# Position bias lines written to DRAM once, read back as overlapping reversed rows and flipped by a matmul

## The chip, the core and the metric

The kernel runs on one core of a Trainium2 chip. The metric is the time of one execution on the device in microseconds (us). The engines of the core work side by side, each through its own queue in order: TensorE (matmuls; PE in the rows, its weight loads PEld), VectorE (DVE), ScalarE (ACT), GpSimd (POOL) and SyncE (SP), which here only issues transfers. Sixteen DMA engines move the data between DRAM, which holds inputs, output and scratch, and the on-chip memory SBUF. Matmul results land in PSUM, eight banks of 128 x 512 float32.

## What is computed

One decoder layer on 512 tokens of width 1024. A modulated layer norm feeds one wide input projection. From it come a gated MLP branch and three groups of eight attention heads, with windows and strides of (128, 1), (512, 4) and (2048, 16). The branches are merged by gates, projected and normalized, and a mixture of 32 experts, four for each token, follows. The part that matters here is the position bias of the attention: it depends on the distance of query and key alone.

```python
band = (didx >= 0) & (didx <= span)                 # didx = qi + 128 - ki
bucket = t5_bucket(jnp.clip(didx, 0, None) * dilation)
bias = bias_table[bucket].astype(jnp.float32).transpose(2, 0, 1)
logits = einsum('brnqhd,brnkhd->brnhqk', qb, kb) * (Dh ** -0.5) + bias
logits = where(valid, logits, NEG_INF)
...
p = exp(logits - m)
o = einsum('brnhqk,brnkhd->brnqhd', p / den, vb)
```

## The kernel before

The program consists of a front (about the first 650 us) and the experts. In the front, the modulation vectors are computed from `w_ada`, the normalized input is transposed and split into two float32r parts (`hh`, `hl`), and every projection is done as three float32r matmuls (`mm3`, L165 to L167). Weights come as tiles of 1 MB (`wload`, L114, pool `land`, four buffers, issued by SP). ScalarE and VectorE split each tile into two halves (L109 and L110, pool `splA`, four buffers).

For each head group g, `attention(g)` projects v, k and q (`projN`, `projT`). Four PSUM accumulators named `mm` collect a projection and are emptied into `t2` tiles: v and q by ScalarE (L480), k by VectorE (L482). Between these projections of the groups 1 and 2, `mod_row` (L451) computes a modulation row: four tiles of `w_ada`, each multiplied and added on VectorE (L221 and L223 in `mod_acc`), then two plain float32 matmuls with a column of ones (L457).

Then the heads are worked off. A step j takes `nh` heads: 2 of width 256 in group 0, 4 of width 128 in the others, so that there are 4, 2 and 2 steps, eight in all. Each step needs one bias tile of 128 queries x 512 values. For each of four blocks of queries, TensorE computes scores (L510) in one of two PSUM tiles named `at`, VectorE scales them and adds the bias (L513), takes the maximum (L515), ScalarE takes the exponential (L519), TensorE transposes (L524), VectorE copies (L526), TensorE multiplies by v (L532) and ScalarE copies out (L534).

The bias is a Toeplitz matrix, a line of values for each head read at an offset that moves by one from query to query. The lines (`fv`: 8 heads, 383 values in group 0 and 255 in the others) come from one small matmul per group (L426) and a copy (L428). L429, issued by GpSimd, writes each line 128 times to the DRAM scratch `toep`, one copy per query. `bias_tile` (L431) then reads with SP (L435): query p starts at copy p and goes back by p values, so that a row pitch of n - 1 gives the slanted read. A bias tile has two buffers, and VectorE reads it at L513.

The order of each queue is not written out by hand here. A planner of the framework fixes it at build time, from program order as priority, from dependences and free buffers, and from modelled durations. On the chip each engine then keeps to that order, whatever the real durations are. Loads of weights, bias tiles and rows share the SP queue.

The experts run in a schedule by hand: for each expert twelve 1 MB tiles of weights pass through 17 buffers, some of which are those that the front gives back (`land`, `landB`, `splA`).

Of the kernel before, what the change touches and what calls it, by code (L numbers as in the profile page):

```python
# [9 lines left out]
F32 = mybir.dt.float32  # L10
# [11 lines left out]
P = 128  # L22
# [4 lines left out]
NE = 32  # L27
# [5 lines left out]
SEGS = (383, 255, 255)  # L33
# [4 lines left out]

def host_consts():

    cst = np.zeros((P, 3 * P + NE), np.float32)
    cst[:, :P] = np.eye(P)
    cst[:, P:2 * P] = np.arange(P)
    cst[:, 2 * P:3 * P] = np.triu(np.ones((P, P)), 1)
    cst[:, 3 * P:] = 8.0 ** (np.arange(NE) % 8)
    edges = np.array([16, 22, 30, 40, 54, 73, 99, 134, 182, 246, 332, 450, 609, 825, 1117, 1513])

    def bucket(d):
        return d if d < 16 else 15 + int((edges <= d).sum())

    oh = np.zeros((33, sum(SEGS)), np.float32)
    for g, n in enumerate(SEGS):
        for u in range(n):
            t = u - 127
            if g == 0:
                d = P - t if 0 <= t <= P else -1
            elif g == 1:
                d = -4 * t if t <= 0 else -1
            else:
                d = -4 * t if t <= 0 and t % 4 == 0 else -1  # L60
            if d < 0:
                oh[32, SEG0[g] + u] = NEG
            else:
                oh[bucket(d), SEG0[g] + u] = 1.0
    sel = np.concatenate([np.eye(NE, dtype=np.float32)] * 3, 0)
    return {"cst": cst, "ohb": oh, "sel": sel}


def layer(tc, I, out, dump=None, n_exp=NE):
    nc = tc.nc  # L70
    V, S, G, PE, SP = nc.vector, nc.scalar, nc.gpsimd, nc.tensor, nc.sync
    main = ExitStack()
    dram = main.enter_context(tc.tile_pool(name="dram", bufs=1, space=DRAM))
# [5 lines left out]
    rowd = dram.tile([4, D], F32, name="rowd")  # L79
    h2d = dram.tile([T, D], F32, name="h2d")  # L80
    ysum = dram.tile([T, D], F32, name="ysum")
    toep = [dram.tile([8, P, n], F32, name=f"toep{g}") for g, n in enumerate(SEGS)]

    cst = cp.tile([P, 2 * P], F32, name="cst_s")
    SP.dma_start(cst, I["cst"][:, :2 * P])
# [26 lines left out]
    def wload(ap, pool=None, eng=SP):  # L112
        t = (pool or land).tile([P, 2048], F32, name="land")
        eng.dma_start(t.rearrange("p (k f) -> p k f", k=ap.shape[1]), ap)  # L114
        return t
# [57 lines left out]
    f = fa.enter_context(tc.tile_pool(name="f", bufs=1, side="right"))  # L173
# [14 lines left out]
    def att():  # L188
        return pA.tile([P, 512], F32, name="at", bufs=2)
# [51 lines left out]
    pb = att()  # L241
# [140 lines left out]
    pb = att()  # L382
# [25 lines left out]
    for g in range(8):  # L408
        ps = pot()
        PE.matmul(ps[:, :256].rearrange("p (n c) -> p n c", n=4), wsT[:, g], vn[:, :, 64 * g:64 * g + 64],  # L410
                  start=True, stop=True)
# [11 lines left out]
    for g in range(3):  # L423
        n = SEGS[g]
        ps = att()
        PE.matmul(ps[:8, :n], relb[:, 8 * g:8 * g + 8], ohb[:, SEG0[g]:SEG0[g] + n], start=True, stop=True)  # L426
        fv = f.tile([8, 512], F32, name="t2", bufs=22)
        S.copy(fv[:, :n], ps[:8, :n])  # L428
        G.dma_start(toep[g], fv[:, None, :n].to_broadcast([8, P, n]))  # L429

    def bias_tile(g, h0, nh, w):  # L431

        t = f.tile([P, nh, w], F32, name="bias", bufs=2)
        n = SEGS[g]
        SP.dma_start(t, bass.AP(tensor=toep[g].tensor, offset=toep[g].offset + h0 * P * n + 127,  # L435
                                ap=[[n - 1, P], [2 * P * n, nh], [1, w]]))
        return t

    yaT = b16(F32R, 2, 4, T)
# [27 lines left out]
    def attention(g, between=()):  # L467
# [27 lines left out]
        for j in range(8 // nh):  # L495

            h0 = j % 2 + 2 * nh * (j // 2)
            hs = slice(h0, h0 + 2 * nh - 1, 2)
            bt = bias_tile(g, h0, nh, w)
            for b in range(4):  # L500
                kb0 = 1 if g == 0 and b == 0 else 0
# [158 lines left out]
    f = fb.enter_context(tc.tile_pool(name="f2", bufs=1, side="right", reuse_waits="tile"))  # L660
# [10 lines left out]
    for a in range(4):  # L671
        t = wload(wov[:, 2 * a:2 * a + 2, :])
# [30 lines left out]
    tri = f.tile([P, P], F32, name="pj", bufs=2)  # L703
    SP.dma_start(tri, I["cst"][:, 2 * P:3 * P])
    pow8 = f.tile([P, NE], F32, name="pow8")
    SP.dma_start(pow8, I["cst"][:, 3 * P:])
    iota_e = iota[:, :NE]
    V.tensor_copy(trib, tri)
    oneb = f.tile([P, P], BF, name="oneb")
# [668 lines left out]
```

## Time and profile before

| | |
|---|---|
| timed runs, median (range) | 1897.74 us (1893.63 to 1898.98), 3 runs |
| profiled execution, its time | 1892.72 us |
| its span, first to last instruction | 1891.0 us |
| TensorE busy | 1740.1 us (92%) |
| VectorE, ScalarE, GpSimd busy | 547.4, 378.2, 203.4 us |
| moved by DMA | 518.99 MB, 274 GB/s in the mean |
| mean granted clock of TensorE | 0.968 of full speed |

The span is cut into 40 slices of 47.3 us on the page; a digit is the busy share of a slice in tenths. The granted clock (PEclk) is what TensorE was given of its full speed. Waits are listed as waiter, releaser, total, times, longest. A plain float32 matmul stands in the rows as two records, a float32r matmul as one. The rows show single executions, so that a duration in them may differ by a little from run to run.

### The profile page before, as it was taken

The numbers are of one execution on the slowest core, as the hardware profiler recorded it, in microseconds if no ns is written. First come the engines' busy times: TensorE is split into PE (matmuls) and PEld (weight loads), VectorE is DVE, ScalarE is ACT, GpSimd is POOL, SyncE is SP. The second block draws the span as 40 slices with busy tenths as digits, with TensorE's granted clock in tenths as the row PEclk, the third lists the DMA queues.
The fourth block names the chain that finished last, engine by engine and source line by source line (L and its number), as shares of the span: only waits on it lengthen the run. The fifth ranks groups of instructions, "written<-read, shape, count | busy, mean of one in ns | idle before, by whom it ended". The sixth has DMA issues, their size and how long they took to land. (4 is left out here: it accounts for less than half of the span.)

```text
span 1891.0 us, 20283 instructions
## 1 busy us (share of the span) xinstructions
PE 1740.1 (92%) x7574; PEld 989.6 (52%) x7574; DVE 547.4 (29%) x901; ACT 378.2 (20%) x737; POOL 203.4 (11%) x152
## 2 busy tenths in 40 slices
PE   5993999999999699999999999998899999999985
PEld 5773878888777444444444444443344444444442
DVE  7532654845267801111111111111101111111115
ACT  3530434444555310011000000010010000000001
POOL 2100000003122410010000000010000001001002
PEclk9997999999999699999999999999999999999998
DMA  8595522723225897999999999999972499949993
GB/s 282 185 94 149 206 88 81 257 69 108 93 99 174 279 379 260 361 404 405 396 399 401 371 393 378 352 400 400 404 286 88 160 393 394 388 160 327 405 372 139
DMA packets 160475, 518.99 MB, mean 274 GB/s; under 512 B 19018, under 2 KB 23426, under 8 KB 160198
## 3 DMA queue, kind: packets, MB, share of 16 engines
q1 hardware_dynamic: 146886, 490.68, 67.7%
q0 software_dynamic: 13312, 24.98, 7.3%
q8 instruction: 129, 2.11, 0.5%
q14 instruction: 148, 1.21, 0.2%
HBM read 504.15 MB, written 26.64 MB: 281 GB/s over the span
## 5 line engine op out<-in xcount | busy, mean ns | idle before, releaser
L165 PE MATMUL mm<-b,splA 128*128 128x512 f32 x352 | 139.5, 396 | 28.7 <-DVE t L482 28.7
L1079 ACT ACTIVATE ga<-ga 128x512 f32<-128x512 f32 (+1 forms) x36 | 28.7, 796 | 576.9 <-DVE ga L1078 400.8
L1131 PE MATMUL po<-land,aT 128*128 128x512 f32 x320 | 141.5, 594 | 1.1 <-DVEq L1173 1.1
L166 PE MATMUL mm<-b,splA 128*128 128x512 f32 x352 | 139.0, 395 | 0.0
L167 PE MATMUL mm<-b,splA 128*128 128x512 f32 x352 | 138.6, 394 | 0.0
L1105 PE MATMUL pu<-land,xT 128*64 128x256 f32 x1024 | 123.9, 386 | 6.3 <-DMA land<-in_w_up_dram 6.3
L1108 PE MATMUL pu<-land,xT 128*128 128x512 f32 x288 | 128.8, 592 | 0.0
L1073 PE MATMUL pg<-land,xT 128*128 128x512 f32 x288 | 126.0, 592 | 2.4 <-issue 2.4
L110 DVE TENSOR_TENSOR splA<-land,splA 128x1024 fp32r<-128x1024 f32 x70 | 87.9, 1258 | 129.0 <-ACT splA L109 124.6
L1070 PE MATMUL pg<-land,xT 128*64 128x512 f32 x504 | 118.9, 619 | 4.1 <-DMA land<-in_w_gate_dram 2.9
L1078 DVE TENSOR_SCALAR ga<-pg 128x512 f32<-128x512 f32 x44 | 30.4, 692 | 318.1 <-PE pg L1073 154.9
L1082 DVE TENSOR_SCALAR pu<-pu 128x256 f32<-128x256 f32 (+1 forms) x64 | 34.1, 533 | 290.5 <-PE pu L1108 160.9
L109 ACT CAST splA<-land 128x1024 fp32r<-128x1024 f32 x72 | 75.3, 1052 | 213.1 <-PE mm L167 171.9
L1128 PE MATMUL po<-land,aT 128*64 128x512 f32 x448 | 105.1, 607 | 7.6 <-ACT aT L1089 7.6
L1089 ACT COPY aT<-ptm 128x256 f32<-128x256 f32 (+1 forms) x64 | 28.9, 452 | 350.6 <-PE ptm L1039 350.6
L1105 PEld LDWEIGHTS pu<-land,xT 128*64 128x64 f32 x1024 | 72.9, 138 | 47.8 <-DMA land<-in_w_up_dram 9.6
L1131 PEld LDWEIGHTS po<-land,aT 128*128 128x128 f32 x320 | 59.4, 190 | 70.3 <-issue 67.9
L1026 POOL DMA_INDIRECT xrow<-h2d,gidx x32 | 33.9, 1060 | 538.3 <-PE ptm L1039 528.3
L1073 PEld LDWEIGHTS pg<-land,xT 128*128 128x128 f32 x288 | 54.6, 190 | 69.2 <-issue 66.3
L165 PEld LDWEIGHTS mm<-b,splA 128*128 128x128 f32 x352 | 66.6, 189 | 44.6 <-DVE t L482 29.1
L1108 PEld LDWEIGHTS pu<-land,xT 128*128 128x128 f32 x288 | 53.5, 190 | 66.1 <-issue 63.9
L1070 PEld LDWEIGHTS pg<-land,xT 128*64 128x64 f32 x504 | 38.2, 143 | 75.3 <-issue 66.7
(376 smaller groups left out, 2498.9 us busy)
## 6 DMA issues: line engine op xcount, KB each, us to landing
land<-in_w_up_dram SPq DMA_DIRECT2D x100, 1024.0 KB
land<-in_w_gate_dram SPq DMA_DIRECT2D x99, 1024.0 KB
land<-in_w_down_dram SPq DMA_DIRECT2D x96, 1024.0 KB
splA<-in_w_down_dram SPq DMA_DIRECT2D x32, 1024.0 KB
land<-in_w_in_dram SPq DMA_DIRECT2D x30, 1024.0 KB
splA<-in_w_gate_dram SPq DMA_DIRECT2D x29, 1024.0 KB
splA<-in_w_up_dram SPq DMA_DIRECT2D x28, 1024.0 KB
land<-in_w_ada_dram SPq DMA_DIRECT2D x24, 1024.0 KB
```

Source lines behind the costliest of these rows:

```text
L109: hi = S.copy(w[:, 0], src)
L110: return hi, eng.tensor_tensor(w[:, 1], src, w[:, 0].bitcast(F32), op=ALU.subtract)
L165: PE.matmul(o, l[0], r[0], start=start, stop=False)
L166: PE.matmul(o, l[0], r[1], start=False, stop=False)
L167: return PE.matmul(o, l[1], r[0], start=False, stop=stop)
L1070: PE.matmul(r[h], x[:, kt, :H], w[:, :, h], start=False, stop=kt == KT - 1)
L1073: PE.matmul(o[st], x[:, kt], w[:, 512 * st:512 * st + 512], start=False, stop=kt == KT - 1)
L1082: V.tensor_scalar(o, o, LIMIT, -LIMIT, op0=ALU.min, op1=ALU.max)
L1105: PE.matmul(o[st][H * h:H * h + H, :256], x[:, kt, :H], w[:, 256 * h:256 * h + 256], start=False, stop=kt == KT - 1)
L1108: PE.matmul(o[st], x[:, kt], w, start=False, stop=kt == KT - 1)
L1128: end = PE.matmul(o[0][H * n:H * n + H], a[:, 2 * st + b, H * h:H * h + H], wn, start=ft == 0, stop=ft == KT - 1)
L1131: end = PE.matmul(o[n], a[:, ft], wn, start=ft == 0, stop=ft == KT - 1)
```

## The change

The lines are written to `toep` once: the scratch is `[8, n]` instead of `[8, 128, n]`. `bias_tile` reads 128 overlapping rows, partition p starting at value p of the line, so the slant runs the other way and the queries stand in reverse order. A matmul with a reversed identity (`flip`, a new 64 KB constant that SP loads) brings them into order: from the tile to a PSUM tile of the `at` kind, from which ScalarE copies back into the same tile. The host constant `cst` gets 128 more columns for it. Each of the eight bias tiles thus has one more plain float32 matmul and one more ScalarE copy between its read and its readers.

```diff
--- before.py
+++ after.py
@@ -38,11 +38,12 @@
 
 def host_consts():
 
-    cst = np.zeros((P, 3 * P + NE), np.float32)
+    cst = np.zeros((P, 4 * P + NE), np.float32)
     cst[:, :P] = np.eye(P)
     cst[:, P:2 * P] = np.arange(P)
     cst[:, 2 * P:3 * P] = np.triu(np.ones((P, P)), 1)
-    cst[:, 3 * P:] = 8.0 ** (np.arange(NE) % 8)
+    cst[:, 3 * P:3 * P + NE] = 8.0 ** (np.arange(NE) % 8)
+    cst[:, 3 * P + NE:] = np.eye(P)[::-1]
     edges = np.array([16, 22, 30, 40, 54, 73, 99, 134, 182, 246, 332, 450, 609, 825, 1117, 1513])
 
     def bucket(d):
@@ -79,7 +80,7 @@
     rowd = dram.tile([4, D], F32, name="rowd")
     h2d = dram.tile([T, D], F32, name="h2d")
     ysum = dram.tile([T, D], F32, name="ysum")
-    toep = [dram.tile([8, P, n], F32, name=f"toep{g}") for g, n in enumerate(SEGS)]
+    toep = [dram.tile([8, n], F32, name=f"toep{g}") for g, n in enumerate(SEGS)]
 
     cst = cp.tile([P, 2 * P], F32, name="cst_s")
     SP.dma_start(cst, I["cst"][:, :2 * P])
@@ -426,14 +427,19 @@
         PE.matmul(ps[:8, :n], relb[:, 8 * g:8 * g + 8], ohb[:, SEG0[g]:SEG0[g] + n], start=True, stop=True)
         fv = f.tile([8, 512], F32, name="t2", bufs=22)
         S.copy(fv[:, :n], ps[:8, :n])
-        G.dma_start(toep[g], fv[:, None, :n].to_broadcast([8, P, n]))
+        G.dma_start(toep[g], fv[:, :n])
+
+    flip = f.tile([P, P], F32, name="flip")
+    SP.dma_start(flip, I["cst"][:, 3 * P + NE:])
 
     def bias_tile(g, h0, nh, w):
 
+        n = SEGS[g]
         t = f.tile([P, nh, w], F32, name="bias", bufs=2)
-        n = SEGS[g]
-        SP.dma_start(t, bass.AP(tensor=toep[g].tensor, offset=toep[g].offset + h0 * P * n + 127,
-                                ap=[[n - 1, P], [2 * P * n, nh], [1, w]]))
+        SP.dma_start(t, bass.AP(tensor=toep[g].tensor, offset=toep[g].offset + h0 * n, ap=[[1, P], [2 * n, nh], [1, w]]))
+        pb = att()
+        PE.matmul(pb, flip, t.rearrange("p h w -> p (h w)"), start=True, stop=True)
+        S.copy(t.rearrange("p h w -> p (h w)"), pb)
         return t
 
     yaT = b16(F32R, 2, 4, T)
@@ -703,7 +709,7 @@
     tri = f.tile([P, P], F32, name="pj", bufs=2)
     SP.dma_start(tri, I["cst"][:, 2 * P:3 * P])
     pow8 = f.tile([P, NE], F32, name="pow8")
-    SP.dma_start(pow8, I["cst"][:, 3 * P:])
+    SP.dma_start(pow8, I["cst"][:, 3 * P:3 * P + NE])
     iota_e = iota[:, :NE]
     V.tensor_copy(trib, tri)
     oneb = f.tile([P, P], BF, name="oneb")
```

## Rows read from the trace of the kernel before

**Rows 1.** The page, part 2: busy tenths in 40 equal slices of the span.

```profile
PE   5993999999999699999999999998899999999985
...
DMA  8595522723225897999999999999972499949993
```

**Rows 2.** Stretches of 10 us: length, busy us by engine, PEclk, DMA.

```profile
150.00:160.00 10.00, 0.00 (x0) 0.00 (x0) 0.00 (x0) 0.00 (x0) 0.00 (x0) 0.50 0.50 65
160.00:170.00 10.00, 0.00 (x0) 0.00 (x0) 0.00 (x0) 0.00 (x0) 0.00 (x0) 0.50 0.49 102
170.00:180.00 10.00, 7.43 (x25) 6.03 (x26) 5.55 (x7) 1.05 (x1) 0.00 (x0) 0.69 0.53 178
```

**Rows 3.** Waits of TensorE, longest: waiter, releaser, us in total, times, longest.

```profile
PE mm L165 <- DVE t L482: 28.7, 1, 28.7
```

**Rows 4.** Timeline of all engines around the hole: start us, us, what.

```profile
138.00 1.28 DVE L482 COPY t<-mm 128x512 f32<-128x512 f32 x2
...
143.50 0.39 PE L167 MATMUL mm<-b,splA 128*128 128x512 f32 x1
171.16 0.75 DVE L221 TENSOR_SCALAR q<-land,cs 128x1024 f32<-128x1024 f32 x1 [31.88 <-DMA land<-in_w_ada_dram]
...
172.56 0.80 PE L165 MATMUL mm<-b,splA 128*128 128x512 f32 x1 [28.68 <-DVE t L482]
...
176.42 0.40 PE L165 MATMUL mm<-b,splA 128*128 128x512 f32 x1
...
176.65 0.39 PE L166 MATMUL mm<-b,splA 128*128 128x512 f32 x1
...
178.73 1.28 DVE L223 SCALAR_TENSOR_TENSOR q<-land,cs,q 128x1024 f32<-128x1024 f32 x1 [3.29 <-DMA land<-in_w_ada_dram]
```

**Rows 5.** Timeline of the SP queue: issues of transfers.

```profile
132.67 0.37 SPq L114 DMA_DIRECT2D land<-in_w_ada_dram  x1
...
173.73 0.37 SPq L114 DMA_DIRECT2D land<-in_w_ada_dram  x1
...
231.94 0.37 SPq L435 DMA_DIRECT2D bias<-toep  x1
...
569.25 0.43 SPq L684 DMA_DIRECT2D row_ln_g<-in_ln_g_dram  x1
```

**Rows 6.** Transfers by issue: tile, queue, count, KB each, us to landing.

```profile
toep<-t POOLq DMA_DIRECT2D x2, 1020.0 KB, 65.7
toep<-t POOLq DMA_DIRECT2D x1, 1532.0 KB, 55.3
```

**Rows 7.** The toep tiles: their issues, and the landing of the three writes.

```profile
L429 POOL DMA_DIRECT2D toep<-t x3: 1079/1113/1337, 91.2 to 93.6; - x3
...
DMA to landing us min/median/max: 55.3/56.5/74.9
```

**Rows 8.** Longer stretches: two in the attention, one in the experts.

```profile
200.00:250.00 50.00, 50.00 (x257) 41.58 (x257) 35.50 (x62) 22.51 (x71) 0.00 (x0) 1.00 0.40 138
300.00:350.00 50.00, 49.95 (x270) 44.73 (x269) 34.03 (x49) 32.16 (x90) 1.01 (x2) 1.00 0.28 87
900.00:1000.00 100.00, 98.65 (x427) 43.55 (x426) 13.48 (x22) 8.20 (x15) 8.14 (x7) 1.00 1.02 397
```

**Rows 9.** Timeline of TensorE around a plain float32 matmul.

```profile
373.97 1.88 PE L457 MATMUL at<-q,ones 128*1 128x512 f32 x4
375.78 0.50 PE L165 MATMUL mm<-b,splA 128*128 128x512 f32 x1
```

**Rows 10.** Timeline of ScalarE: one copy of 128x512 from PSUM.

```profile
115.37 0.59 ACT L480 COPY t<-mm 128x512 f32<-128x512 f32 x1 [0.30 <-PE mm L167]
```

**Rows 11.** Stretches with a bias read alone, and with broadcast lines.

```profile
233.00:234.00 1.00, 1.00 (x5) 0.61 (x5) 1.00 (x3) 0.18 (x1) 0.00 (x0) 1.00 0.80 240
570.00:575.00 5.00, 5.00 (x19) 3.97 (x19) 2.16 (x4) 0.00 (x0) 0.00 (x0) 0.78 0.86 295
```

**Rows 12.** Timeline of VectorE: first reader of the bias tile issued at 231.94.

```profile
245.85 0.42 DVE L513 SCALAR_TENSOR_TENSOR sc<-at,bias 128x256 f32<-128x256 f32 x1
```

## Prediction

> **What bounds the kernel now.** I read the views in this order: busy shares and slices, stretches of 10 us, waits of TensorE, the timeline around the one hole, then the transfers. The slices show one hole in TensorE, the fourth slice, about 142 to 189 us, while the DMA engines go on working [rows 1]. By stretches TensorE does nothing from 150 to 170 us and is back at 170 to 180 us with a mean granted clock of 0.69 of full speed [rows 2]. The wait list names it: one wait of 28.7 us, a matmul of the next projection for the copy at L482, the largest of TensorE's list [rows 3].
>
> The timeline shows the cause [rows 4]. VectorE empties two of the four k accumulators from 138.00 on. The next instruction in its queue is L221, the first step of a modulation row, which needs a w_ada tile; it starts at 171.16 after 31.88 us of idling for that transfer. Two further L482 copies stand behind L221, so the accumulators stay full. TensorE starts its last matmul at 143.50 and the next at 172.56. The w_ada tile was issued at 132.67 [rows 5], so it took 38.5 us. The next one, issued at 173.73 [rows 5], is read at 178.73 [rows 4], 5.0 us later. What differed is the traffic: the three toep writes (one of 1532 KB, two of 1020 KB [rows 6]) were issued from 91.2 to 93.6 and took 55.3 to 74.9 us [rows 7]; if the longest is the last one, it was done near 168.5. While only they and the w_ada tile remain, the DMA engines show a share of 0.49 to 0.50 and move 65 to 102 GB/s [rows 2]. About 3 us after the last toep byte the w_ada tile is there. So the 128-fold write does not delay the bias itself; it delays a weight tile, which delays VectorE's queue, which delays TensorE.
>
> Behind the hole TensorE is full again (50.00 and 49.95 us of two later stretches of 50 us [rows 8]), and it is not catching up: the work behind it moves by what the hole costs. The expert stage later has TensorE at 98.65 of 100 us with a DMA share of 1.02 [rows 8]; its tiles are loaded into buffers that the earlier stages give back, so its start moves with them. I therefore carry the whole gain to the end.
>
> **The change part by part.**
> *Toep writes.* 3.57 MB become 24 lines of 1020 or 1532 bytes, 28 KB in all, and the long traffic goes. The w_ada tile of 132.67 should then land after about 5.0 us, at 137.7, before L221 comes up at 139.28 (two copies, 1.28 us, from 138.00). The slack is 1.6 us. What comes next is VectorE's wait for the second w_ada tile, 3.29 us before 178.73 [rows 4]; it exists already, TensorE ran beside it, and it stays hidden. So the 28.68 us wait goes.
> *Clock.* In the idle stretch the granted clock falls to 0.50 [rows 2], the lower of its two levels (1.2 against 2.4 GHz). From 172.56 to 176.42 nine matmuls start some 0.43 us apart, and behind them the step is 0.23 us [rows 4]. 3.86 minus 9 times 0.23 is 1.8 us. Gone as well. Together 30.5 us.
> *Flip matmuls, 8.* A plain float32 128x512 matmul is two records on TensorE. Two of them at L457 hold it from 373.97 to 375.78 [rows 9], 0.90 us each. L457 has one column of weights and the flip 128, but weight loads run beside the stream. 8 times 0.90 is 7.2 us, and as TensorE is full there [rows 8], all of it counts. Lower bound 0 (if they fall into other idle time, of which there is little), upper bound 8 times 1.0 us, since the matmul behind the change of operand takes 0.50 instead of 0.39 us [rows 4, 9], 8.0 us.
> *ScalarE copies, 8.* PSUM to SBUF, 128x512: 0.59 us [rows 10], 4.7 us in all. ScalarE is busy 22.51 and 32.16 of 50 us in the stretches concerned [rows 8], so I cost them at nothing. The cover is TensorE's projection matmuls; without it, a score step would start 0.59 plus 0.90 us later for each tile, 12 us over eight.
> *The at buffers.* pb takes one of the two PSUM buffers of the scores from matmul to copy, about 1.5 us a tile. A score step that waits for it costs TensorE nothing while projection matmuls are there to run; between 0 and 8 times 1.5 = 12 us, and I take 1 us, near the lower end, because TensorE is full in these stretches with the same two buffers [rows 8].
> *Bias reads, 8.* Same bytes (256 KB) and row lengths as before. One alone, issued at 231.94 [rows 5], shows as 240 GB/s in the microsecond from 233 to 234 us [rows 11], which is nearly all of its 256 KB; its first reader starts at 245.85 [rows 12]. Slack some 12 us; flip and copy use 1.5 of it. I cost it at nothing.
> *Other.* The flip constant is one more 64 KB load on SP, whose issues take about 0.4 us [rows 5]; the three GpSimd issues stay. Nothing there ends a wait.
>
> The reads now overlap: 128 partitions read rows that begin 4 bytes apart in one line. The nearest rows are the norm lines read by all partitions from one 4 KB row, issued from 569.25 on [rows 5]; from 570 to 575 us the DMA engines move 295 GB/s [rows 11], so many readers of one small region are not slow here.
> The Trainium skill (DMA: Bandwidth & Descriptors, Latency and other measured facts) tells of HBM row pitches that halve the rate, with aliasing of channels inferred; by it a bias read might take twice its 1 us. That stays within the slack of 12 us and would add nothing to the sum; only where a flip stands directly behind its read would it count (third rival below). No row here shows such a loss.
>
> **The sum.** The profiled execution took 1892.7 us (span 1891.0). 1892.7 - 28.7 - 1.8 + 7.2 + 1.0 = 1870.4. The three timed runs have a median of 1897.7, 5.0 above it, and the mean of all four is 1895.8, 3.1 above. I place the forecast between both bases: 1872, about 1.3% faster.
>
> **The rivals.**
> 1. *A new wait on TensorE, small.* Each queue is ordered at build time by a planner, and TensorE works in order. A flip queued before its bias tile has landed stops the projections behind it, where before only VectorE waited for the tile. A wait of 1 to 2 us per tile is 8 to 16 us: 1880 to 1888. For it: the order of all queues is made anew, and the L221 row shows what a wrong guess costs. Against it: slacks of 12 us and more.
> 2. *The hole remains.* If the w_ada tile is late for another reason (the SP queue, VectorE's order), only the flips come on top: 1895.8 + 8.2 = 1904. Against it: the second w_ada tile landed in 5.0 us.
> 3. *Slower: the flip as a toll on every tile.* Place: TensorE's queue, just ahead of each flip. Price: the whole landing of a bias read. At the 65 GB/s of the stretch with toep traffic [rows 2] 256 KB takes about 4 us, plus 1 us for issue and semaphores, 5 us a tile, 40 us in all: 1872 + 40 = 1912. It decides from about 3 us of exposed wait per tile, where 8 waits eat the 30.5 - 8.2 us left. Against it: 240 GB/s in the row of one read alone.
> 4. *More gain.* The lines are there at about 95 instead of 147 us, so bias loads and scores can be ordered earlier and the flips partly fall in small gaps; the ceiling is the whole 30.5 us: 1862 to 1866.
>
> **How the numbers follow.** Forecast (1866 to 1879) 0.60; rival 1 0.20; rival 2 0.05; rival 3 0.06; rival 4 0.09. The range takes rival 4 and rival 1 in and leaves out 2 and 3: 1861 to 1889. A measurement of this kernel can tell about 0.3%, 5.7 us, from no change, that is 1890 to 1901. Faster gets the forecast, rival 4 and nearly all of rival 1: 0.85. Within 0.3%: the long end of rival 1 and a mild form of rival 3, 0.07. Slower: rival 2 and the rest of rival 3, 0.08.
>
> **What would show it.** Right: no wait of TensorE above 5 us between 130 and 180 us, granted clock 1.00 there, toep landing in single microseconds, w_ada landing in about 5 us, 16 records for the flip line at about 0.45 us from start to start, and the expert stage starting some 22 us earlier. Wrong: L221 or another VectorE step still waiting for w_ada with L482 behind it; waits of TensorE on bias transfers at the flip line; VectorE waiting at L513 for the copies; or the front ending 22 us earlier and the expert stage not.

## The result, and the profile after

The changed kernel takes 1882.86 us in the median (22 runs, 1877.76 to 1892.02), the kernel before 1897.41 us beside it (22 runs); the ratio is 0.9934, with a 95% interval of 0.9921 to 0.9946. It is faster, as forecast in sign, by 14.5 us in the medians and by 12.5 by the ratio. The time lies in the range, but the gain is only about half of the 25.5 us between 1897.4 and the forecast of 1872. The profiled execution took 1887.25 us (span 1885.5), 4.4 above its median; that of the kernel before lay below its own median. So spans are compared only stage by stage.

The tile toep, after: the loads of the bias tiles, then the three writes, and last the time from issue to landing (answers to [rows 7]).

```profile
L439 SPq DMA_DIRECT2D bias<-toep x8: 360/367/461, 90.8 to 311.9; - x8
L430 POOL DMA_DIRECT2D toep<-t x3: 526/554/769, 88.9 to 90.3; - x3
...
DMA to landing us min/median/max: 1.9/4.6/4.8
```

The writes land within single microseconds, where they took 55.3 to 74.9. Stretches after, answers to [rows 2] and [rows 8]; columns are the stretch and its length, busy us (instructions) of PE, PEld, DVE, ACT and POOL, granted clock, DMA share, GB/s.

```profile
100.00:150.00 50.00, 50.00 (x223) 41.23 (x223) 22.23 (x29) 14.35 (x17) 0.00 (x0) 1.00 0.32 109
150.00:200.00 50.00, 50.00 (x229) 39.23 (x228) 32.98 (x51) 20.80 (x56) 0.00 (x0) 1.00 0.61 203
...
280.00:290.00 10.00, 10.00 (x61) 8.74 (x61) 5.57 (x12) 5.65 (x26) 0.00 (x0) 1.00 0.31 112
290.00:300.00 10.00, 10.00 (x39) 7.92 (x38) 4.19 (x8) 3.21 (x16) 0.00 (x0) 0.57 0.07 16
300.00:310.00 10.00, 10.00 (x37) 8.02 (x36) 1.98 (x3) 3.96 (x16) 0.00 (x0) 0.50 0.00 0
310.00:320.00 10.00, 10.00 (x50) 9.27 (x48) 8.58 (x11) 7.48 (x20) 0.00 (x0) 0.91 0.11 29
```

The hole is gone: TensorE is busy 50.00 of 50 us twice, at full clock. But in the attention of group 1 the granted clock falls to 0.50, the lower level (1.2 GHz), and the matmuls done in 10 us fall from 61 to 37, while the busy column still says 10.00 of 10. The flip and its copy (durations in ns, least, median and largest; then who waited, us and times):

```profile
L441 PE MATMUL at<-bias,flip x16: 591/592/595, 160.4 to 391.6; 128*128 128x512 f32 x16
...
who waited for it (us, times):
  ACT bias L442: 3.9, 4
```

Nobody but ScalarE's copy waits for a flip, and TensorE's waits after show none for a bias tile.

To place the rest I compared the two traces record by record: the start of the n-th 512-wide projection matmul in both. Just behind the old hole the kernel is 33.0 us ahead, 2.4 of which it already had before the hole (a low clock at 40 us, longer in the execution before); the hole and its low clock were thus worth 30.7. Behind group 0's four flips it is 27.7 ahead, at the middle of group 1's attention 17.3, behind group 2 14.4, at the first matmul of the experts (into `pg`, the accumulators of the gate projection) 14.3, and at the end of the two profiled spans 5.5. So the loss has two places beside the flips: about 8 us in group 1, and about 9 us in the experts, whose instructions the change doesn't touch.

### The profile page after: what moved, and what is told of

Its sections match the earlier page's. It is cut to its first block, busy times and chain, and to the rows that moved or that the text cites. A ratio compares the mean times of both kernels' runs of the same rounds, so it can differ in the third digit from the quotient of the medians.

```text
span 1885.5 us, 20333 instructions
## 1 busy us (share of the span) xinstructions
PE 1757.6 (93%) x7590; PEld 999.1 (53%) x7590; DVE 547.0 (29%) x901; ACT 383.1 (20%) x745; POOL 201.9 (11%) x152
## 5 line engine op out<-in xcount | busy, mean ns | idle before, releaser
L1111 PE MATMUL pu<-land,xT 128*64 128x256 f32 x1024 | 129.1, 395 | 8.4 <-DMA land<-in_w_up_dram 8.4
```

Source lines behind the costliest of these rows:

```text
L1111: PE.matmul(o[st][H * h:H * h + H, :256], x[:, kt, :H], w[:, 256 * h:256 * h + 256], start=False, stop=kt == KT - 1)
```

## The experiments

All times are medians; differences to the kernel before are to its runs beside the same kernels. The runs come from three sets, in which the median of the kernel before was 1898.1, 1896.8 and 1895.4 us, so a difference of 2 or 3 us between sets says nothing. My theory at first: the long writes made the hole, the flips cost what I forecast, and the missing gain is the low clock in group 1, which comes of the flip's place in TensorE's order. Rivals: the order of queues rather than the writes made the hole; the flips as such cost more; the loss lies in the experts.

**The 128-fold writes back, flips kept.**

```
         G.dma_start(toep[g], fv[:, :n])
+        G.dma_start(wide[g], fv[:, None, :n].to_broadcast([8, P, n]))
```

> The changed kernel, and behind each write of the bias lines the 128-fold write of the kernel before into memory that nobody reads; flips and new order stay. If the long writes made the hole of the kernel before, it comes back: one wait of TensorE of about 25 to 30 us between 140 and 180 us, w_ada landing late, and the time is 25 to 31 us above the changed kernel, 1908 to 1914 us. If the hole came from the order of the queues or from the late lines themselves, the time stays within 5 us of 1883.

1911.2 us, ratio to before 1.0075 (1.0059 to 1.0091), 28.3 above the changed kernel. TensorE's largest wait and VectorE's step behind the late tile:

```profile
PE mm L167 <- DVE t L490: 29.5, 1, 29.5
```

```profile
172.38 0.75 DVE L223 TENSOR_SCALAR q<-land,cs 128x1024 f32<-128x1024 f32 x1 [32.75 <-DMA land<-in_w_ada_dram]
```

This is [rows 3] and [rows 4] again, with the useless traffic added to the changed kernel's own order. Of the three short writes the quickest landed after 1.9 us, but the others, which share GpSimd's queue with the long ones, after 28.5 and 55.0. No wait of the hole is for a bias line: VectorE waits for the w_ada tile. So the traffic of the long writes makes the hole, without the help of the old order.

**Flips in the kernel before.**

```
+        pb = att()
+        PE.matmul(pb, ident, t.rearrange("p h w -> p (h w)"), start=True, stop=True)
+        S.copy(t.rearrange("p h w -> p (h w)"), pb)
```

> The kernel before (128-fold write, rows read slanted, no reversal), to which each bias tile gets one identity matmul and one ScalarE copy: the price of the flips alone, with the hole left in place. By the terms of my sum alone: 7.2 us of matmuls and 1 us at the buffers, 1905 to 1906 us, and TensorE's granted clock stays at 1.00 in the attention of group 1 (270 to 360 us). If the flip inside the stage also leaves a stretch of narrow matmuls in which the granted clock falls (my theory for the missing 8 us), a low clock of some 20 us stands in that attention and the time is 1912 to 1917 us. If the missing gain lies elsewhere (in the experts), the first.

1917.35 us, ratio 1.0113 (1.0094 to 1.0132), 19.2 above before, more than either expectation, and no low clock in group 1. Record by record, the flips are as forecast: from just ahead of them (4.9 behind the kernel before) to just behind group 2 (12.8) the eight cost 7.9 us. The 4.9 us ahead of them are early stretches of low clock and a hole of 30.2 us; what sets them I did not try. Another 7 us come in the experts, as in the changed kernel. So the flips' price stands, the rival that they cost more falls, and the experts are a place of loss that my theory had not.

**Both tiles of a group flipped ahead of its steps.**

```
+        tiles = [bias_tile(g, j, nh, w) for j in range(2)] if g else None
...
-            bt = bias_tile(g, h0, nh, w)
+            bt = tiles[j] if g else bias_tile(g, h0, nh, w)
```

> The changed kernel with both bias tiles of groups 1 and 2 loaded and flipped before the first step of the group, so that no flip and copy stands between the score steps of a group. If the second flip and its copy in the middle of the stage are what let the granted clock fall in group 1, the low clock of 20 us there goes and the time is 6 to 9 us below the changed kernel, 1874 to 1877 us. If the low clock comes from the flips' work as such or from the earlier attention, it stays and the time is within 3 us of 1883.

1881.41 us, ratio 0.9912 (0.9895 to 0.9928).

```profile
290.00:300.00 10.00, 10.00 (x60) 7.93 (x59) 4.19 (x8) 6.31 (x30) 0.00 (x0) 1.00 0.11 27
```

The low clock is gone and the projections end 9.2 us earlier than in the changed kernel's profile, as the theory says; but the median falls by 1.5 us only, and the intervals of the two ratios overlap. Half a miss: the timed runs do not show the low clock to be the main part of the missing gain.

**No flips: the lines stored back to front.**

```
-                oh[bucket(d), SEG0[g] + u] = 1.0
+                oh[bucket(d), SEG0[g] + n - 1 - u] = 1.0
...
-                V.scalar_tensor_tensor(scv, sv, 0.125, bt[:, :, w - wv:], op0=ALU.mult, op1=ALU.add)
+                V.scalar_tensor_tensor(scv, sv, 0.125, bass.AP(tensor=bt.tensor, offset=bt.offset + wv - 1,
+                    ap=[bt.ap[0], [w, nh], [-1, wv]]), op0=ALU.mult, op1=ALU.add)
```

> The changed kernel without flips: the lines are stored back to front by the table that makes them, so a tile read as overlapping rows has its partitions in the right order and only its free dimension reversed, which VectorE's bias step reads with a step of -1. No flip load, matmul or copy. If my terms hold, the hole stays away (30.5 us), the 7.2 and about 2 us of flips go, and with them the low clock in group 1: 1862 to 1867 us. If VectorE reads backwards more slowly, its bias step, 0.6 us for 128x512 now, would double and the attention would end later: 1870 to 1880. If the low clock comes from the earlier attention and not from flips, about 8 us are missing: 1872 to 1875.

1866.13 us (1865.74 to 1868.52), ratio 0.9843 (0.9827 to 0.9858): the best kernel of this study, better than both. The bias step that reads backwards, here and in the changed kernel, where it reads forwards:

```profile
L513 DVE SCALAR_TENSOR_TENSOR sc<-at,bias x32: 414/682/693, 162.3 to 393.5; 128x512 f32<-128x512 f32 x28, 128x256 f32<-128x256 f32 x4
```

```profile
L519 DVE SCALAR_TENSOR_TENSOR sc<-at,bias x32: 413/681/692, 163.3 to 408.8; 128x512 f32<-128x512 f32 x28, 128x256 f32<-128x256 f32 x4
```

Reading backwards costs nothing (682 against 681 ns). Behind the old hole this kernel is 30.7 us further ahead than in front of it, against the 30.5 of my hole and clock terms; the last projection starts 30.1 us earlier than before, and the median gains 32.0. There is no low clock between 200 and 560 us, and the experts take about as long as before: 1239.3 us from their first matmul into `pg` to the end, against 1237.5. In the changed kernel they take 1246.4, in the two kernels above 1244.6 and 1249.6, in the one with the traffic 1246.1. The experts are scheduled by hand, with the same order of TensorE in all. What differs is how many instructions stand in front of them.

**A second theory, for the experts.** The waits of TensorE that end by nothing the profile shows, in the changed kernel and in the one without flips:

```profile
PE pg L1041 <- issue: 12.2, 3, 5.3
...
PE pg L1079 <- issue: 5.4, 2, 3.4
...
PE ptm L1045 <- issue: 2.1, 1, 2.1
```

```profile
PE pg L1035 <- issue: 12.2, 3, 5.4
...
PE pg L1073 <- issue: 2.0, 2, 1.6
```

The expert stage is a chain of branches (one for each expert and for its number of rows). Theory: these waits are the loading of code, and where they fall depends on the place of the experts in TensorE's instruction stream, which the flips move by 37 records (16 matmuls, 16 weight loads, 5 semaphore waits) against the kernel without them. The page lists the code's own transfers (packets, MB, share):

```profile
q8 instruction: 126, 2.06, 0.4%
```

Each packet has 16,384 bytes. The Trainium skill (Runtime: NRT & Kernel Launch, Instruction fetch mechanics) says that each engine's code is streamed in blocks of 16 KiB by a queue of its own, that a boundary is mostly hidden, and that a taken branch to code that isn't there must wait for it; the packets agree in size. Rival: the flips or the low clock shift something else, and useless instructions cost only themselves.

**Useless matmuls ahead of the experts, no flips.** They write one column that nobody reads.

```
     with tc.manual_schedule(engines={ET.PE, ET.Activation, ET.DVE, ET.SP}):
+        for _ in range(8):
+            PE.matmul(po[0][:, :1], ident, ident[:, :1], start=True, stop=True)
         for e in range(E):
```

> The kernel without flips of the last call (1866.1 us), and at the start of the expert stage 8 one-column float32 matmuls whose result nobody uses. They cost about 1 to 2 us themselves and lengthen TensorE's instruction stream by 16 matmuls and 16 weight loads, about what the 8 flips add. In the four kernels with flips the experts took 7 to 10 us longer than in the kernel before, with waits of TensorE for nothing but issue (2.1 us at the transposes of the expert rows, 3.4 us at the gate matmuls) that the two kernels without flips have shorter or not at all. If these waits belong to the place of the instructions in the stream, this kernel shows them too and takes 1871 to 1875 us. If they belong to the flips or to the order of the attention, it takes 1867 to 1869 us and its issue waits are those of the kernel without flips.

> As the run before with 24 matmuls instead of 8: 3 to 5 us for themselves. If the place of the instructions in the stream sets the issue waits, the waits stand at other matmuls of the experts than in the run with 8, and the experts' length differs from both by several us, in either direction. If not, 1869 to 1872 us and the same waits as with none.

1872.81 us (ratio 0.9880, 0.9861 to 0.9899) and 1888.98 us (0.9956, 0.9938 to 0.9973), against 1866.1 with none: 6.7 and 22.9 us. Up to the first gate matmul behind them they cost 0.8 and 7.6 us themselves (this includes that the wait of 5.4 us which stood there is only 3.0 us long now). The rest lies at waits inside the experts. The gate matmul without flips; with 8 useless matmuls; and in the changed kernel's second profile:

```profile
1622.22 1.98 PE L1073 MATMUL pg<-land,xT 128*128 128x512 f32 x4 [1.57 <-issue]
```

```profile
1625.28 2.93 PE L1073 MATMUL pg<-land,xT 128*128 128x512 f32 x3 [3.56 <-issue]
```

```profile
1641.01 2.73 PE L1079 MATMUL pg<-land,xT 128*128 128x512 f32 x3 [3.56 <-issue]
```

Counted from the first matmul into `pg`, and leaving the useless ones out, the kernel with 8 (32 records added) waits at matmuls 1774 (1.6 us) and 3891 (3.6), and the changed kernel (37 records) does at 1774 (1.1) and 3891 (3.4): the same two. All kernels with flips have these two, if nothing else is added. The kernel without flips waits at 2036 (1.1) and 3895 (1.6) instead, and so does the kernel before, which has 4 records more and one more wait, of 3.3 us at 422. With 24 they stand elsewhere, at 1122, 1384, 2870 and 3364, 2.5 to 4.4 us each. Each of the three waits over 4 us there makes the kernel 5.8 to 5.9 us later, with a granted clock of 0.50 in a short stretch behind it. The second theory's numbers for 8 and for the change hold; "several us in either direction" for 24 was 15, more than I expected.

What the waits are for can be read from the packets of the instruction queue, whose start and end the traces hold. In the 14 profiled executions TensorE has 85 waits of at least 0.9 us in the experts that end by nothing the views show (releaser "issue"). All 85 end 1.3 to 1.8 us after a packet of q8 did; a packet takes about 1.1 us, and one comes every 11 us or so, so that 1 in 20 would do this by chance. Of the 229 waits of that length with another releaser, 4 do. These waits are for code, then. They come both at the first gate matmul of an expert, behind the branch to that expert (1122, 1384), and in the middle of a gate, where no branch stands (1774, 3891).

**The copy on VectorE, and the changed kernel once more.**

```
-        S.copy(t.rearrange("p h w -> p (h w)"), pb)
+        V.tensor_copy(t.rearrange("p h w -> p (h w)"), pb)
```

> The changed kernel with the copy of the flipped tile on VectorE instead of ScalarE; the planner then puts projection matmuls between the narrow ones behind the second flip of groups 1 and 2. If the low clock in group 1 comes of the stretch in which TensorE has only narrow matmuls waiting for ScalarE's exponentials, it is gone: no granted clock of 0.50 between 270 and 360 us, the attention of group 1 some 8 us shorter than in the profiled execution of the changed kernel, and a time of 1876 to 1881 us. If it is the flips' own work, or a matter of chance in each execution, the time stays at 1880 to 1886 us.

> The changed kernel as it is, one more profiled execution. If the order alone decides, a granted clock of 0.50 for about 20 us stands in the attention of group 1 again. If each execution draws it anew (the kernel before with flips has the same order of matmuls there and no low clock), it may be missing, and the stage is then 8 to 9 us shorter. The issue waits of the experts should be those of the first profile, 2.1 and 3.4 us, if the instruction stream sets them.

1880.06 us (ratio 0.9923, 0.9896 to 0.9950) with the copy on VectorE, and 1887.69 for the one execution of the changed kernel. The stretches of group 1, first with the copy on VectorE, then the changed kernel:

```profile
290.00:300.00 10.00, 10.00 (x65) 7.98 (x63) 5.46 (x11) 5.99 (x29) 0.00 (x0) 1.00 0.12 29
300.00:310.00 10.00, 10.00 (x54) 9.33 (x55) 8.35 (x12) 8.18 (x21) 0.00 (x0) 1.00 0.11 28
```

```profile
290.00:300.00 10.00, 10.00 (x43) 7.99 (x43) 4.09 (x9) 4.04 (x20) 0.00 (x0) 0.65 0.10 27
300.00:310.00 10.00, 10.00 (x36) 8.00 (x37) 2.13 (x4) 3.64 (x15) 0.00 (x0) 0.50 0.00 0
```

The low clock is there again with the changed kernel's order and not with the other, where the projections end 9.6 us earlier than in the first profile. But the median gains 2.8 us, not 8, with overlapping intervals, and it lies in both of the ranges that I had given. Of the issue waits in the second execution of the changed kernel, the one of 3.4 us is at its place (3.6), but the one of 2.1 us at a transpose is gone, and 1.7 us stand at a later transpose: the short waits are not set by the stream alone.

**Other numbers of useless matmuls, and 16 in the changed kernel.** The edit is the loop above with 4, 16 and 32, and with 16 in the changed kernel.

> The kernel without flips and 4 useless one-column matmuls at the start of the experts. In the run with 8 they took 3.4 us for 16 records, of which the first expert's issue wait, shorter by 2.4 us, took most back; 4 should cost 0 to 1 us themselves. If the place in TensorE's instruction stream decides, the long issue waits stand at other matmuls than in the kernel without any or with 8, and the time lies anywhere from 1862 to 1875 us; if only whole jumps of the stream count (as with 8, like the changed kernel), 1866 to 1868.

> The same with 16: 6.8 us for 32 records less the 2.4 us of the first wait, 4 to 5 us. If only their own time counts, 1870 to 1872 us. If the place decides, the issue waits lie at other matmuls than with 8 or 24, and the time is 1875 us or more.

> The same with 32: some 13.6 us for 64 records less 2.4, 11 us. If their own time is all, and the 23 us of the run with 24 had another cause, the cost grows on with their number: 1889 us or more. If the place decides, the time need not grow with the number: the waits of 4 to 5 us at the first gate matmul of four experts, which the run with 24 showed, are at other places or gone, and the time may be below that of the run with 24.

> The changed kernel with 16 of the useless matmuls at the same place. Its flips and waits already lengthen TensorE's stream by 38 instructions against the kernel without flips; with 64 more it stands where the run with 24 stood (96). If the place in the stream sets the issue waits, this kernel shows the long ones of that run (4 to 5 us at the first gate matmul of several experts) and takes 1895 to 1904 us. If the matmuls cost only their own 4 to 5 us, 1887 to 1888 us.

The kernel without flips, by the number of useless matmuls (what they cost themselves is what the profile shows up to the first matmuls behind them; the rest is the difference):

| number | records added | median us | against none | themselves | rest |
|---|---|---|---|---|---|
| 0 | 0 | 1866.1 | | | |
| 4 | 16 | 1868.7 | 2.6 | 0 | 2.6 |
| 8 | 32 | 1872.8 | 6.7 | 0.8 | 5.9 |
| 16 | 64 | 1880.9 | 14.8 | 4.5 | 10.3 |
| 24 | 96 | 1889.0 | 22.9 | 7.6 | 15.3 |
| 32 | 128 | 1874.3 | 8.2 | 11.3 | -3.1 |

32 of them take 14.7 us less than 24. No price per matmul gives that; a place does. Not all of the rest is waiting for code, though. In the last expert TensorE waits at matmul 4794 for VectorE, whose queue waits for rows of `ysum`: 1.6 us with no useless matmuls, 10.0 with 16 and with 24, 4.9 with 32. VectorE's step, without and with 24:

```profile
1824.42 1.29 DVE L1257 BATCH_NORM_STATS2 fst<-splA 128x6 f32<-128x512 f32 x2 [1.52 <-DMA splA<-ysum]
```

```profile
1852.25 1.29 DVE L1257 BATCH_NORM_STATS2 fst<-splA 128x6 f32<-128x512 f32 x2 [9.33 <-DMA splA<-ysum]
```

This long wait stands in the kernels that lack the two waits for code shortly before (2.6 and 4.2 us, at 4296 and 4558), and in no other; why the rows land late there, no run tries. Record by record, the kernel with 24 is 27.7 us behind the one without any at matmul 4260, 19.0 at 4740 and 27.5 at the end: what the two missing waits gave back is lost again there. The changed kernel with 16 takes 1890.48 us (ratio 0.9985, 0.9966 to 1.0005), 7.6 above the changed kernel, where its own matmuls explain about 4 (with 16 the waits at 4296 and 4558 are gone here too, and 9.1 us stand at 4794); it fell short of the 1895 to 1904 that I expected, but its waits stand where the theory put them. Its added records are 37 and 64, 101; the run with 24 has 96. Two of the long waits with 24, then with the changed kernel and 16:

```profile
896.11 0.64 PE L1035 MATMUL pg<-ball,selb 96*64 96x512 bf16 x2 [4.19 <-issue]
...
971.17 0.64 PE L1035 MATMUL pg<-ball,selb 96*64 96x512 bf16 x2 [4.05 <-issue]
```

```profile
891.27 0.64 PE L1041 MATMUL pg<-ball,selb 96*64 96x512 bf16 x2 [3.97 <-issue]
...
967.78 0.41 PE L1041 MATMUL pg<-ball,selb 96*64 96x512 bf16 x2 [4.28 <-issue]
```

The matmuls 1122, 1384, 2870 and 3364 wait 2.4 to 4.4 us in both kernels, one with flips and one without (the changed one has a fifth, 860). With 16 the long waits are at 1384 and 3626, with 32 at 568, 2286 and 4704, and with 4 they are where they are with none; that time, 0.9857 (0.9837 to 0.9878) of before, can't be told from the 0.9843 without any. The loss in the experts belongs to the place in the stream. The stretch of group 1 in this run, with the changed kernel's own order of the front:

```profile
290.00:300.00 10.00, 10.00 (x62) 8.08 (x60) 4.98 (x10) 5.64 (x26) 0.00 (x0) 1.00 0.10 27
```

No low clock here. Of the five profiled executions with that order of matmuls in group 1 (the changed kernel twice, with the traffic, with 16 useless matmuls, and flips in the kernel before), three show it, 17 to 20 us long, and two do not. Of the nine with other orders (the kernel before, both tiles ahead, copy on VectorE, no flips with 0 to 32 useless matmuls) none has more than 3.4 us of it there. In the first profile the clock falls at 291.3, and from 287.84 to 293.40 TensorE had only matmuls of 64 or 128 columns, which wait for ScalarE's exponentials. So the order seems to allow the low clock, and the executions differ in whether it comes; five executions are few, and what decides is not shown.

## Why the prediction was right and wrong

*Toep writes and clock.* Right, in size too. Forecast 30.5 us; the hole and its clock were worth 30.7 us in the changed kernel and in the kernel without flips, which gains 32.0 in all, and the traffic alone brings a hole of 29.5 us back. The w_ada tile and VectorE's queue were the way, as read from [rows 4] and [rows 5]; no new wait took the hole's place.

*Flip matmuls, copies and at buffers.* Right: 7.2 and 1.0 us forecast, 7.9 measured in the kernel before; the changed order with both tiles ahead ends its front 6.5 us later than the kernel without flips. From the medians at about the same place in the stream (1881.4 and 1880.1 against the 1872.8 with 8 useless matmuls) it is 7.3 to 8.6. ScalarE's copies were hidden.

*Bias reads.* Right: rows that overlap cost nothing that shows, and TensorE waited for no bias tile. The toll on every tile, and the first rival as I described it (a flip waiting for its tile), did not happen, though the time lies in the span that I gave that rival: that it does, and that it lies in my range, is luck, since neither the sum nor a rival had what was lost. Its reason, an order made anew, was half right: the order opened a stretch of narrow matmuls, no wait. The row pitches for which the Trainium skill (DMA: Bandwidth & Descriptors, Latency and other measured facts) has the rate halved are of megabytes; the rows here begin 4 bytes apart, so that note did not bear on these reads.

*"I therefore carry the whole gain to the end."* This is the step that failed. I carried it because TensorE was full in the experts [rows 8] and their tiles go into buffers that the stages ahead give back. They started 14.3 us earlier, not 22, and took some 7 to 9 us longer in the profile, 5.9 by the run with 8 useless matmuls. My sum priced an added instruction by the time that it runs; it put at nothing, without a reason, that it moves all code behind it, in a stage that is made of branches.

*"TensorE is full there [rows 8], so all of it counts."* I read a busy column of 50 as full speed. Group 1 was just as busy after, at half the clock. It costs 8 to 9 us in an execution that has it; in the median of the timed runs the two orders without it gain 1.5 and 2.8, neither clear of the noise, so its share there is not known better than that.

The account of the medians, then: 1866.1 without flips, plus 5.9 to 6.7 for the place, 7.3 to 8.6 for the flips, 1.5 to 2.8 for the low clock: 1880.8 to 1884.2, and 1882.9 is measured. The terms are differences of these same medians, so the sum must come out about right and proves nothing; the flips' 7.9 and the 7 to 9 us in the experts, from the traces, stand apart from it. Against my forecast that is some 6 us of place and some 2 of clock that the sum lacked; about 3 more are my choice of a base between the profiled time and the median (the same terms taken from 1897.4 give 1875.1).

What stays open: what decides in an execution whether the clock falls in group 1; which blocks of code the waits are for, and why a given place makes them long; and why the `ysum` rows land late when two of the waits are gone.

## What to carry to other kernels

When an edit adds instructions to an engine ahead of a stage of branches, its price is not only their run time: look for waits with the releaser "issue" in that stage, see whether each ends just behind a packet of the instruction queue, and try a few harmless instructions in front to see how much the place is worth (here from -3 to 15 us, not all of it at waits for code) before a small difference is put down to the edit. A write that is shared out to 128 copies may cost nothing where it stands and 30 us at a weight tile that shares its DMA engines. And before an order is reversed by an engine, see whether the table that makes the data, or the step of a reader, can hold it for nothing.

## What the runs showed of the hardware

- Reading the second operand of VectorE's multiply-and-add backwards, with a step of -1 inside each head's 128 or 256 columns (512 columns of float32 in all), takes 682 ns against 681 forwards.
- 128 rows that begin 4 bytes apart in one line load without a visible loss: eight such loads, and TensorE waited for none.
- Between 16 and 128 records added to TensorE's stream ahead of the experts, the time went 1868.7, 1872.8, 1880.9, 1889.0 and 1874.3 us. The issue waits of TensorE there, up to 4.3 us in the rows above, end 1.3 to 1.8 us after a packet of 16,384 bytes of the instruction queue. The "mostly hidden" of the Trainium skill for a boundary of a code block (Runtime: NRT & Kernel Launch, Instruction fetch mechanics) does not hold in this stage of branches: 3.6 us stand in the middle of a gate.
- Busy shares do not show the clock: 10.00 of 10 us busy with 61 matmuls at a granted clock of 1.00, and with 37 at 0.50.
